# Down projection of a decoder block as seven-product visits, with the residual summed in HBM

## The chip, the cores and the metric

One core of a Trainium2 chip runs the whole kernel. The metric is device time in microseconds (us); lower is better. All arithmetic is float32 in the reference; on TensorE the kernel works with pairs of rounded float32 ("fp32r") values, hi and lo, whose sum is the number.

## What is computed

A decoder block on 512 tokens of 2048 channels: attention and a convolution branch, then a feed-forward part and a gated input. The change lies in the feed-forward's second product and reaches into the gate that follows it:

```python
h = _rmsnorm(x, g_ffn[l])
u = _causal_dwconv(h @ w_up[l], ffn_conv_w[l], ffn_conv_b[l])
ug, uv = jnp.split(u, 2, axis=-1)
x = x + (jax.nn.silu(ug) * uv) @ w_down[l]          # 512 x 5632 by 5632 x 2048
h = _rmsnorm(x, g_ple[l])
x = x + jax.nn.sigmoid(h @ w_ple_gate[l]) * (p[l].astype(x.dtype) @ w_ple_proj[l])
return _rmsnorm(x, g_final)
```

## The kernel before

Channels lie on the 128 partitions and tokens along the free axis, so a tile `a` is 128 channels x 512 tokens. The hidden layer has 44 such tiles (`hid`, kept in HBM), the residual 16 (`x1d` in HBM, `self.x1` in SBUF). `Kernel.run` takes a list of groups and issues their weight chunks one after the other. For each chunk it loads the raw weights on the SP queue into a pool of 7 buffers (`wraw`), up to 16 us of work ahead (`loads`), and cuts them one or two chunks ahead (`prep`): `cut` makes hi on ScalarE (line 268) and lo, the rest, on VectorE (line 269). `pump` gives the side work (evictions, statistics, hidden tiles) a turn after each chunk. A scheduler then sets the order of each engine's instructions; loads that go through `load` keep the program's order on SP.

An ordinary chunk (`Group`) is 256 rows by 512 columns of the weights: for 2 row blocks and 4 output tiles three matmuls of 512 tokens each, hi by hi, hi by lo and lo by hi (`products`, line 403), 24 in all.

The up projection runs as 44 `Pair`s. A pair is a 2 x 2 block product in seven products instead of eight (the Strassen-Winograd form): halves of the depth by two output tiles by halves of the tokens. `operands` makes the seven right-hand sides from two tiles. Each of them holds hi of 256 tokens in its left half and lo in its right, so a step takes one matmul of 512 columns (line 379) and one of 256 (line 380) per row block, eight row blocks per product. The seven weight operands come from `wraw`, from sums that were made in HBM beforehand (`s`), and from adding a further block by an accumulating transfer of GpSimd's queue (line 306).

The down projection (lines 948 to 951) is plain: four parts of 12, 12, 12 and 8 hidden tiles (`PARTS`), in each of which all 16 output tiles are made in four groups `mg`. `fetch` loads a part's hidden tiles and splits them into hi and lo, the first part beside the last pair, the next parts beside groups of the part before. `ready` loads the residual tiles `self.x1` in the first part; `ev_down` (line 945) adds each part's PSUM to them in SBUF on VectorE. The gate's first group then begins with `split_x1`, which makes hi and lo of every residual tile and the sum of squares, and ends in `stats`, whose result `rb3` the first eviction of the gate needs (line 1003). The last gate group is done in two halves of the tokens, so its matmuls have 256 columns.

Of the kernel before, what the change touches and what calls it, by code (L numbers as in the profile page):

```python
# [1 line left out]

# [15 lines left out]
P = 128  # L18
S = 512
# [40 lines left out]
class Group:  # L60


    def __init__(self, w, rhs, evict, tok=False, before=None, ns=ALL, keep=None):
        self.ns = ns
        self.w, self.rhs, self.evict, self.tok, self.before = w, rhs, evict, tok, before
        self.n = w.shape[0]
        self.nm = w.shape[3] // P
        self.keep = keep


class Pair:
# [9 lines left out]
    def __init__(self, src, rhs, evict, before=None, beside=()):  # L81
        self.src, self.rhs, self.evict, self.before, self.beside = src, rhs, evict, before, iter(beside)
        self.kh = src[1].shape[1]
        self.raw, self.cut, self.ps, self.c = {}, {}, {}, {}


class Kernel:
# [164 lines left out]
    def run(self, groups):  # L252
        nc = self.nc
        chunks = []
        for n, g in enumerate(groups):
            if not isinstance(g, Pair):
                chunks += [(g, c) for c in range(g.n)]
                continue
            if not isinstance(groups[n - 1], Pair):
                chunks.append((g, 5))  # L260
            after = groups[n + 1] if isinstance(groups[n + 1], Pair) else None
            chunks += [(after if p == 5 else g, p) for p in ORDER if p != 5 or after]
# [31 lines left out]
        def prep(i, kks=(slice(0, 2),)):  # L294
# [3 lines left out]
            if isinstance(g, Pair):  # L298
                hi = self.whi.tile([P, g.kh, P], F32R, tag="w", name="whi")
                lo = self.wlo.tile([P, g.kh, P], F32R, tag="w", name="wlo")  # L300
                raw = g.raw[{6: 5, 3: 5}.get(c, c)]
# [20 lines left out]

        loadx = self.start(dma, prep)
        begun.update(range(3))
        cuts = 1
        for i, (g, c) in enumerate(chunks):
# [8 lines left out]
            if g.before and c == (5 if isinstance(g, Pair) else 0):  # L335
                g.before()
            if isinstance(g, Pair):
                self.pair_step(g, c)
                for _ in range(2):
                    next(g.beside, None)  # L340
                self.pump()
                continue
# [10 lines left out]
            if c == g.n - 1:  # L353
                g.evict(g.ps)
            self.pump()
# [12 lines left out]
    def pair_step(self, g, c):  # L368
# [21 lines left out]
        if p == 4:  # L390
            g.evict(g.c[1], g.c[6], g.c[4], g.c[5])

# [237 lines left out]
    def build(self):  # L630
# [223 lines left out]
        def fold(c, eng):  # L854
            eng.tensor_tensor(c[:, LEFT], c[:, LEFT], c[:, RIGHT], op=ALU.add)

# [33 lines left out]
        F0 = [sum(PARTS[:i]) for i in range(len(PARTS))]  # L890
        hs = {}

        def fetch(pi):
            raw = {}
            for f in range(F0[pi], F0[pi] + PARTS[pi] + 2):
                if f < F0[pi] + PARTS[pi]:
                    raw[f] = self.A()
                    self.load(out=raw[f], in_=hid[f])
                if f - 2 >= F0[pi]:
                    hs[f - 2] = self.split(raw.pop(f - 2))  # L900
                yield


# [5 lines left out]

        def sums():  # L910
# [10 lines left out]
        builders = {0: fetch(0)}  # L921
        for j in range(KF):
            groups.append(Pair(srcs[j], lambda p, k: T2[p][k], ev_up(j), before=first_up if j == 0 else None,
                               beside=builders[0] if j == KF - 1 else ()))

        def ready(pi, mg):
            def f():
                if mg == 0:
                    if pi == 0:
                        self.finish_chains()  # L930
                    for _ in builders[pi]:
                        pass
                if pi == 0:
                    for m in range(4 * mg, 4 * mg + 4):
                        self.x1[m] = self.A()
                        self.load(out=self.x1[m], in_=x1d[m])
                if mg == 1 and pi + 1 < len(PARTS):
                    builders[pi + 1] = self.add_bg(fetch(pi + 1))
            return f

        def ev_down(mg):
            def f(ps):
                for m in range(4):
                    z = self.x1[4 * mg + m]
                    nc.vector.tensor_tensor(z, ps[m], z, op=ALU.add)
            return f

        for pi, n in enumerate(PARTS):
            for mg in range(4):
                groups.append(Group(t["w_down"][mg][F0[pi] // 2:(F0[pi] + n) // 2], lambda k, pi=pi: hs[F0[pi] + k],  # L950
                                    ev_down(mg), before=ready(pi, mg)))


        h2, pj = {}, {}

        def split_x1():
            for k in range(KD):
                h2[k] = self.split(self.x1[k], self.col(C_GPLE + k))
                self.nacc = self.square_add(self.x1[k], self.nacc)
                if k % 2:  # L960
                    yield
            yield from stats("rb3")()

        def begin_gate():
            self.g_split = self.add_bg(split_x1())
            next(self.g_split)
            next(self.g_split)

        def load_pj(mg):
            def f():  # L970
                if mg == 0:
                    begin_gate()
# [51 lines left out]
        for mg in range(4):  # L1024
            groups.append(Group(t["w_gate"][mg], lambda k: h2[k], ev_gate2(4 * mg, TOK_A if mg == 3 else ALL),
                                ns=TOK_A if mg == 3 else ALL, keep=kept if mg == 3 else None, before=load_pj(mg)))
        self.again = Group(t["w_gate"][3], lambda k: h2[k], lambda m, ps: ev_gate2(12 + m, TOK_B)([ps]), ns=TOK_B, keep=kept)
# [70 lines left out]
```

## Time and profile before

| | us |
|---|---|
| median of three runs | 2794.7 (2792.41 to 2795.51) |
| the profiled run, its own time | 2794.55 |
| span of that run, in which the engines work | 2792.8 |
| up projection, about | 1242 to 2108 in the span |
| down projection, about | 2108 to 2590 |
| gate, about | 2590 to 2779 |

TensorE (PE in the profile) is busy 99% of the span, VectorE (DVE) 62%, ScalarE (ACT) 41% and GpSimd (POOL) 6%. PEld is the loading of weights into TensorE, which runs beside its matmuls. Busy shares are means over unlike stages, so the stretches have to be read apart. The mean duration of one matmul is not what it costs, since each starts before the one ahead has ended; the price is the time of a long unbroken piece divided by its count. "Granted clock" is the part of TensorE's full speed that it had.

### The profile page before, as it was taken

To read this page: it belongs to the slowest core of one execution; us is meant where nothing else is said; L and a number is where in the kernel's file an instruction comes from. 1 tells how busy PE (TensorE), PEld (TensorE's weight loads), DVE (VectorE), ACT (ScalarE), POOL (GpSimd) and SP (SyncE) were. 2 spreads that over 40 slices of the span, in tenths; PEclk is the share of its full clock that TensorE was granted. 3 is DMA by queue.
4 is the path that set the end of the run, shared out by engine and by line. 5 is a ranking of instruction groups with operands and counts; after the bars stand their busy time and mean duration, and the time that the engine had idled before them with its cause. 6 is when DMAs were issued, how large, how long until landed. Compare 5 with 4: busy or idle time off the path is not lost.

```text
span 2792.8 us, 34852 instructions
## 1 busy us (share of the span) xinstructions
PE 2758.9 (99%) x13528; PEld 2323.2 (83%) x13528; DVE 1732.3 (62%) x2554; ACT 1138.2 (41%) x1647; POOL 166.2 (6%) x200
## 2 busy tenths in 40 slices
PE   9999999999999999999999999999999999999997
PEld 7888888888888888878888888888887888888787
DVE  5464588658646354478788887878876333335436
ACT  5354452222124233355555555555554221213323
POOL 0010110000000000000000000000000000000000
PEclk9999999999999999999999999999999999999998
DMA  8575756676666754366767676767666343323322
GB/s 275 162 226 141 225 149 195 195 197 183 195 195 190 197 156 162 147 203 183 212 190 209 193 206 192 208 198 198 206 198 249 121 143 102 124 94 110 98 95 95
DMA packets 152982, 489.84 MB, mean 175 GB/s; under 512 B 17136, under 2 KB 21232, under 8 KB 152816
## 3 DMA queue, kind: packets, MB, share of 16 engines
q1 hardware_dynamic: 127328, 395.32, 39.9%
q0 software_dynamic: 25344, 92.29, 18.8%
q8 instruction: 106, 1.74, 0.2%
q14 instruction: 60, 0.49, 0.1%
q10 hardware_dynamic: 144, 0.01, 0.0%
HBM read 457.14 MB, written 116.39 MB: 205 GB/s over the span
## 4 chain that ended last, share of the span: by engine, by line
PE 95%; DMA 2%; DVE 1%; ACT 1%; issue 0%; SPq 0%; POOL 0%; POOLq 0%; DVEq 0%; ACTq 0%
PE m L403 63%; PE m L379 20%; PE m L380 10%; DMA wraw<-w_up 1%; PE x L539 1%; PE x L512 0%; DMA wraw<-w_down 0%; PE x L513 0%; DVE wlo L269 0%; PE x L530 0%; ACT whi L268 0%; DMA wraw<-w_in 0%; SPq L116 0%; DVE o L1018 0%; DMA wraw<-w_proj 0%
## 5 line engine op out<-in xcount | busy, mean ns | idle before, releaser
L403 PE MATMUL m<-a,whi 128*128 128x512 f32 (+1 forms) x5056 | 1547.7, 388 | 11.0 <-ACT whi L268 5.0
L268 ACT ACTIVATE whi<-wraw 128x1024 fp32r<-128x1024 f32 (+1 forms) x637 | 667.8, 1057 | 1437.4 <-PE m L403 912.2
L269 DVE TENSOR_TENSOR wlo<-wraw,whi 128x1024 fp32r<-128x1024 f32 (+1 forms) x637 | 773.7, 1221 | 755.3 <-ACT whi L268 720.9
L403 PEld LDWEIGHTS m<-a,whi 128*128 128x128 f32 x5056 | 945.8, 188 | 203.1 <-ACT whi L268 5.4
L403 PE MATMUL m<-a,wlo 128*128 128x512 f32 (+1 forms) x2528 | 978.7, 388 | 0.0
L379 PE MATMUL m<-a,whi 128*128 128x512 f32 x2464 | 873.9, 400 | 3.5 <-ACT a L383 2.3
L380 PE MATMUL m<-a,wlo 128*128 128x256 f32 x2464 | 693.3, 281 | 0.8 <-DVE wlo L269 0.8
L379 PEld LDWEIGHTS m<-a,whi 128*128 128x128 f32 x2464 | 464.6, 189 | 120.4 <-ACT a L383 3.1
L403 PEld LDWEIGHTS m<-a,wlo 128*128 128x128 f32 x2528 | 475.8, 188 | 97.4 <-DVE wlo L269 1.1
L380 PEld LDWEIGHTS m<-a,wlo 128*128 128x128 f32 x2464 | 467.2, 190 | 1.3 <-DVE wlo L269 1.1
L596 DVE SCALAR_TENSOR_TENSOR a<-a,par 128x485 f32<-128x485 f32 (+19 forms) x240 | 172.4, 734 | 6.1 <-ACT a L593 1.6
L875 DVE SCALAR_TENSOR_TENSOR a<-a,par 128x511 f32<-128x511 f32 (+1 forms) x176 | 131.4, 747 | 1.7
L306 POOL DMA_DIRECT2D wraw<-w_up x88 | 76.3, 868 | 920.9 <-DVE a L868 712.9
L918 POOL DMA_DIRECT2D s<-w_up x88 | 72.7, 826 | 888.2 <-DMA s<-w_up 888.2
L383 ACT ACTIVATE a<-m 128x512 f32<-128x512 f32 x176 | 101.6, 578 | 0.4 <-PE m L380 0.4
L389 DVE TENSOR_TENSOR a<-m,a 128x512 f32<-128x512 f32 x44 | 30.4, 692 | 88.3 <-PE m L380 88.3
L403 PE MATMUL m<-whi,a 128*128 128x512 f32 x256 | 81.3, 392 | 0.0
L873 ACT ACTIVATE a<-a,par 128x512 f32<-128x512 f32 x88 | 71.0, 806 | 8.8 <-DVE a L870 8.0
L146 ACT ACTIVATE a<-a 128x512 fp32r<-128x512 f32 x88 | 53.8, 623 | 41.6 <-DVE a L224 21.6
L147 DVE TENSOR_TENSOR a<-a 128x512 fp32r<-128x512 f32 x88 | 59.3, 686 | 9.2 <-ACT a L146 9.0
L213 POOL TENSOR_TENSOR sm<-sm,mhalf 128x4 f32<-128x4 f32 (+1 forms) x14 | 15.4, 1102 | 804.5 <-DVE sm L212 797.1
L870 DVE TENSOR_TENSOR a<-a 128x512 f32<-128x512 f32 x88 | 60.2, 684 | 0.1
(132 smaller groups left out, 1274.9 us busy)
## 6 DMA issues: line engine op xcount, KB each, us to landing
wraw<-w_in SPq DMA_DIRECT2D x143, 512.0 KB, 4.5
wraw<-w_up SPq DMA_DIRECT2D x132, 512.0 KB, 6.6
s<-w_up SPq DMA_DIRECT2D x88, 512.0 KB, 5.7
s<-w_up POOLq DMA_DIRECT2D x88, 512.0 KB, 7.4
wraw<-s SPq DMA_DIRECT2D x88, 512.0 KB, 5.4
wraw<-w_up POOLq DMA_DIRECT2D x88, 512.0 KB, 6.1
wraw<-w_down SPq DMA_DIRECT2D x88, 512.0 KB, 3.5
wraw<-w_o SPq DMA_DIRECT2D x32, 512.0 KB, 6.9
```

The source lines that it names most:

```text
L268: nc.scalar.activation(hi, w, AF.Copy)
L269: nc.vector.tensor_tensor(lo, w, hi.bitcast(F32), op=ALU.subtract)
L306: nc.gpsimd.dma_start(out=raw, in_=g.src[{5: 1, 6: 2}[c]], accum_op=ALU.add)
L379: nc.tensor.matmul(ps, lhsT=hi[:, k], rhs=t, start=new and k == 0, stop=False, skip_group_check=True)
L380: nc.tensor.matmul(ps[:, LEFT], lhsT=lo[:, k], rhs=t[:, LEFT], start=False, stop=k == g.kh - 1, skip_group_check=True)
L383: nc.scalar.activation(x, ps, AF.Copy)
L403: nc.tensor.matmul(out, lhsT=l, rhs=r, start=first and n == 0, stop=last and n == 2)
L596: nc.vector.scalar_tensor_tensor(y[:, s:], u[:, :S - s], self.col(w + k), y[:, s:], op0=ALU.mult, op1=ALU.add)
L870: nc.vector.tensor_tensor(u, u, rb, op=ALU.mult)
L873: nc.scalar.activation(y, u, AF.Identity, scale=self.col(w + 2), bias=self.col(C_FB + ch))
L875: nc.vector.scalar_tensor_tensor(y[:, s:], u[:, :S - s], self.col(w + 2 - s), y[:, s:], op0=ALU.mult, op1=ALU.add)
L918: nc.gpsimd.dma_start(out=src[n], in_=w[h], accum_op=ALU.add)
```

## The change

The first six hidden tiles (`F0`) stay a plain product, in four groups of three chunks. The other 38 make 19 pairs of row blocks (`KP`), and for them the down projection is done in seven products. Eight pairs of output tiles (`o`) are visited in turn, and a visit takes its pair of outputs over a range of the 19 (`ENDS`, `VISITS`); the number of pairs in the range is called its depth below. There are 26 visits: a first round of depths 2, 3, 4, 5, 6, 7, 8, 8, the first three of them behind the second, third and fourth plain group, a second of depths 7 (seven times) and 8, a third of 8, 8, 8, 7, 6, 5, 4, 3, and at the end two of depth 2 and 1. The operands of a pair (`feed`, through the same `operands`) are made just before the first visit that needs them.

A visit's seven products (`NARROW`: 1, 5, 6, 2, 7, 3, 4) have outputs of 256 tokens, so `visit_step` issues three matmuls of 256 columns for each pair: hi by hi, hi by lo, lo by hi. The four weight blocks of the range are loaded, three sums are made by VectorE (lines 324, 326 and 328 of the changed kernel), and the last sum, for product 3, by an accumulating transfer on GpSimd's queue after product 6 has been cut (line 332). Products 1, 5, 6 and 4 are evicted by ScalarE and 2, 7 and 3 by VectorE.

The residual is no longer kept in SBUF. The plain groups (`ev_plain`, line 1024) and every visit but the last of each output pair (line 1055) add their result to `x1d` in HBM by accumulating transfers on GpSimd's queue, 16 and 36 of 256 KB. The last visit of a pair loads `x1d`, adds it (line 1044), splits the result for the gate and adds its squares (`chain`). The gate takes its rows in the order in which these visits end (`GATE_K`), and `stats` begins with the gate. The hooks of `fetch` and `feed` run with a delay of `LAG` steps.

```diff
-PARTS = [12, 12, 12, 8]
+F0 = 6
+KP = (KF - F0) // 2
+ENDS = [[2, 3, 4, 5, 6, 7, 8, 8], list(range(9, 17)), [min(n, KP) for n in range(17, 25)], [KP] * 2]
+VISITS = [(o, ENDS[r - 1][o] if r else 0, e) for r, es in enumerate(ENDS) for o, e in enumerate(es)]
+GATE_K = [m for o in (2, 3, 4, 5, 6, 7, 0, 1) for m in (2 * o, 2 * o + 1)]
+NARROW = [1, 5, 6, 2, 7, 3, 4]
...
+                if isinstance(g, Pair) and not g.wide:
+                    for h in {1: (0,), 5: (2, 3), 2: (1,)}.get(c, ()):
+                        g.raw[h] = self.wraw.tile([P, g.kh, P], F32, tag="w", name="wraw")
+                        self.load(out=g.raw[h], in_=g.src[h])
+                    return
...
+                if not g.wide:
+                    a = g.raw
+                    if c == 5:
+                        a["s"] = self.wraw.tile([P, g.kh, P], F32, tag="w", name="wraw")
+                        nc.vector.tensor_tensor(a["s"], a[2], a[3], op=ALU.add)
+                    elif c == 6:
+                        nc.vector.tensor_tensor(a["s"], a["s"], a[0], op=ALU.add)
+                    elif c == 7:
+                        nc.vector.tensor_tensor(a[2], a[2], a[0], op=ALU.add)
+                    cut(hi, lo, a[{1: 0, 2: 1, 7: 2, 4: 3}.get(c, "s")])
+                    g.cut[c] = hi, lo
+                    if c == 6:
+                        nc.gpsimd.dma_start(out=a["s"], in_=g.src[1], accum_op=ALU.add)
+                    return
...
+    def visit_step(self, g, c):
+        nc, p = self.nc, c
+        name = {1: "b", 6: "b", 7: "b", 4: "b", 2: "a", 5: "c", 3: "c"}[p]
+        new = name not in g.ps
+        if new:
+            g.ps[name] = self.mm.tile([P, S], F32, tag="m", name="m")
+        ps = g.ps[name][:, :H]
+        hi, lo = g.cut.pop(p)
+        for k in range(g.kh):
+            t = g.rhs(p, k)
+            for n, (w, x) in enumerate(((hi, LEFT), (hi, RIGHT), (lo, LEFT))):
+                nc.tensor.matmul(ps, lhsT=w[:, k], rhs=t[:, x], start=new and k == n == 0, stop=k == g.kh - 1 and n == 2,
+                                 skip_group_check=True)
+        if p in (1, 5):
+            g.c[p] = self.A()
+        if p in (1, 6, 5):
+            nc.scalar.activation(g.c[1 if p == 6 else p][:, LEFT if p == 1 else RIGHT], ps, AF.Copy)
+        elif p in (2, 3):
+            z = g.c[1][:, LEFT if p == 2 else RIGHT]
+            nc.vector.tensor_tensor(z, ps, z, op=ALU.add)
+        elif p == 7:
+            z = g.c[5][:, RIGHT]
+            nc.vector.scalar_tensor_tensor(z, ps, -1.0, z, op0=ALU.mult, op1=ALU.subtract)
+        else:
+            nc.scalar.activation(g.c[5][:, LEFT], ps, AF.Copy, scale=-1.0)
+            g.evict(g.c[1], g.c[5])
...
+        def ev_plain(mg):
+            def f(ps):
+                for m, x in enumerate(ps):
+                    z = self.A()
+                    nc.scalar.activation(z, x, AF.Copy)
+                    nc.gpsimd.dma_start(out=x1d[4 * mg + m], in_=z, accum_op=ALU.add)
+            return f
...
-                    z = self.x1[4 * mg + m]
-                    nc.vector.tensor_tensor(z, ps[m], z, op=ALU.add)
...
+            def before():
+                if end:
+                    for m in ms:
                         self.x1[m] = self.A()
                         self.load(out=self.x1[m], in_=x1d[m])
+            def chain(zs):
+                for m, z in zip(ms, zs):
+                    x = self.x1[m]
+                    nc.vector.tensor_tensor(x, z, x, op=ALU.add)
+                    h2[m] = self.split(x, self.col(C_GPLE + m))
                     yield
+                    self.nacc3 = self.square_add(x, self.nacc3)
+                    yield
+            def evict(*zs):
+                if end:
+                    self.chain(chain(zs))
+                else:
+                    for m, z in zip(ms, zs):
+                        nc.gpsimd.dma_start(out=x1d[m], in_=z, accum_op=ALU.add)
...
-                    begin_gate()
+                    self.finish_chains()
+                    self.nacc = self.nacc3
+                    self.g_split = self.add_bg(stats("rb3")())
```

The SP queue, where the last hidden tile is stored (`hid_17952` before, `hid_17916` after; `hid_11075` and so on are earlier hidden tiles, `x1d` residual tiles). Before:

```order
L116 DMA wraw<-w_down 128x1024
L116 DMA a<-hid_11819 128x512
L116 DMA a<-hid_12005 128x512
L116 DMA wraw<-w_down 128x1024
L116 DMA hid_17952<-a 128x512
L116 DMA a<-x1d_8346 128x512
L116 DMA a<-x1d_8353 128x512
L116 DMA a<-x1d_8688 128x512
L116 DMA a<-x1d_8695 128x512
L116 DMA wraw<-w_down 128x1024 x6
```

After:

```order
L126 DMA wraw<-w_down 128x1024 x3
L126 DMA hid_17916<-a 128x512
L126 DMA a<-hid_11075 128x512
L126 DMA a<-hid_11261 128x512
L126 DMA a<-hid_11447 128x512
L126 DMA a<-hid_11633 128x512
L126 DMA wraw<-w_down 128x1024 x2
```

The four residual loads behind the store are gone, hidden tiles for the new operands stand there instead, and three weight chunks now go out together ahead of it.

VectorE at the same place, from the last of the up projection's convolution on (the product that is stored is line 880 before and 944 after; 177 to 180 and 171, 174 are lines of `operands`). Before:

```order
L875 SCALAR_TENSOR_TENSOR a<-a,par 128x511
L875 SCALAR_TENSOR_TENSOR a<-a,par 128x510
L880 TENSOR_TENSOR a<-a 128x512
L269 TENSOR_TENSOR wlo<-wraw,whi 128x1024 x5
L945 TENSOR_TENSOR a<-m,a 128x512 x4
```

After:

```order
L944 TENSOR_TENSOR a<-a 128x512
L177 TENSOR_TENSOR a<-a 128x256
L178 TENSOR_TENSOR a<-a 128x256
L179 TENSOR_TENSOR a<-a 128x256
L180 TENSOR_TENSOR a<-a 128x256
L171 TENSOR_TENSOR a<-a 128x256 x3
L174 SCALAR_TENSOR_TENSOR a<-a 128x256
L171 TENSOR_TENSOR a<-a 128x256 x2
L177 TENSOR_TENSOR a<-a 128x256
L179 TENSOR_TENSOR a<-a 128x256
L171 TENSOR_TENSOR a<-a 128x256
L178 TENSOR_TENSOR a<-a 128x256
```

Behind the product stood the cuts of the next weight chunks; now 15 instructions on the operands stand there, of which these are the first 14, and the next cut (line 283) behind them.

GpSimd's queue where the up projection ends, before, and in the second round of visits, after (line 332 is the weight accumulate of a visit, 1055 the residual of the visit ahead of it). Before, these are the last rows of the queue:

```order
L213 TENSOR_TENSOR sm<-sm,mhalf 128x4
L306 DMA wraw<-w_up 128x1024 x85
L213 TENSOR_TENSOR sm<-sm,mhalf 128x4
L213 TENSOR_TENSOR sm<-sm,mhalf 128x2 x2
L1093 UNCONDITIONAL_BRANCH
L1093 ISA
```

After:

```order
L1055 DMA x1d_9377<-a 128x512
L1055 DMA x1d_8346<-a 128x512
L1055 DMA x1d_8353<-a 128x512
L332 DMA wraw<-w_down 128x896
L1055 DMA x1d_8688<-a 128x512
L1055 DMA x1d_8695<-a 128x512
```

Where GpSimd had no transfer left after the up projection, a weight accumulate now stands behind two residual accumulates in each visit.

VectorE at the end of the down projection (before: lines 150 and 248 split and square the residual in the gate's first chunks; after: the visit of depth 2, with 1044, 160 and 258 the residual of the visit before, 452 the eviction of that visit's product 3, 324 to 328 the sums). Before:

```order
L269 TENSOR_TENSOR wlo<-wraw,whi 128x1024 x2
L945 TENSOR_TENSOR a<-m,a 128x512 x3
L150 SCALAR_TENSOR_TENSOR a<-a,par 128x512
L945 TENSOR_TENSOR a<-m,a 128x512
L269 TENSOR_TENSOR wlo<-wraw,whi 128x1024
L248 TENSOR_TENSOR a<-a 128x512
L150 SCALAR_TENSOR_TENSOR a<-a,par 128x512
```

After:

```order
L452 TENSOR_TENSOR a<-m,a 128x256
L328 TENSOR_TENSOR wraw<-wraw 128x256
L283 TENSOR_TENSOR wlo<-wraw,whi 128x256
L1044 TENSOR_TENSOR a<-a 128x512
L326 TENSOR_TENSOR wraw<-wraw 128x256
L1044 TENSOR_TENSOR a<-a 128x512
L160 SCALAR_TENSOR_TENSOR a<-a,par 128x512
L283 TENSOR_TENSOR wlo<-wraw,whi 128x256
L258 TENSOR_TENSOR a<-a 128x512
L283 TENSOR_TENSOR wlo<-wraw,whi 128x256
L160 SCALAR_TENSOR_TENSOR a<-a,par 128x512
L283 TENSOR_TENSOR wlo<-wraw,whi 128x256
```

The residual's additions, splits and squares, which stood among cuts of 1024 elements, now stand among cuts and sums of 256 and 128.

## Rows read from the trace of the kernel before

**Rows 1.** The page: busy time of TensorE, and the chain by engine.

```profile
PE 2758.9 (99%) x13528; PEld 2323.2 (83%) x13528; DVE 1732.3 (62%) x2554; ACT 1138.2 (41%) x1647; POOL 166.2 (6%) x200
...
PE 95%; DMA 2%; DVE 1%; ACT 1%; issue 0%; SPq 0%; POOL 0%; POOLq 0%; DVEq 0%; ACTq 0%
```

**Rows 2.** Stretches of up and down projection (columns in the first line).

```profile
core 0: us, PE busy (x) PEld busy (x) DVE busy (x) ACT busy (x) POOL busy (x), PEclk, DMA share, GB/s
1640.00:1740.00 100.00, 100.00 (x568) 86.73 (x567) 80.36 (x106) 56.40 (x72) 8.65 (x10) 1.00 0.69 198
2140.00:2240.00 100.00, 100.00 (x442) 82.80 (x442) 38.71 (x43) 25.74 (x31) 0.00 (x0) 1.00 0.47 166
2440.00:2540.00 100.00, 100.00 (x443) 82.83 (x442) 35.40 (x38) 23.75 (x26) 0.00 (x0) 1.00 0.29 96
```

**Rows 3.** TensorE's waits, 1242 to 2098 us: releaser, total, times, longest.

```profile
PE m L379 <- ACT a L383: 2.3, 1, 2.3
PE m L379 <- ACT whi L268: 1.2, 1, 1.2
PE m L380 <- DVE wlo L269: 0.8, 1, 0.8
```

**Rows 4.** Chain (start, us, what, matmuls); then weight loads, ns least/median/most.

```profile
825.20 38.08 PE m L403 x168
...
2762.00 13.56 PE m L403 x113
...
L403 PEld LDWEIGHTS m<-a x192: 186/192/193, 2727.0 to 2772.3; 128*128 128x128 f32 x192
```

**Rows 5.** Timeline at the change from up to down, chain piece, then stretches.

```profile
2121.90 0.69 DVE L880 TENSOR_TENSOR a<-a 128x512 f32<-128x512 f32 x1
...
2122.62 0.32 SPq L116 DMA_DIRECT2D hid<-a  x1
2123.03 1.82 SPq L116 DMA_DIRECT2D a<-x1d  x4
2124.91 3.51 SPq L116 DMA_DIRECT2D wraw<-w_down  x6
...
2124.91 5.51 DMA wraw<-w_down
...
2131.62 1.22 PE L403 MATMUL m<-a,whi 128*128 128x512 f32 x2 [4.97 <-ACT whi L268]
...
2131.59 5.11 DVE L269 TENSOR_TENSOR wlo<-wraw,whi 128x1024 fp32r<-128x1024 f32 x4 [9.00 <-ACT whi L268]
...
2132.00:2136.00 4.00, 3.96 (x10) 2.62 (x10) 3.79 (x4) 2.98 (x3) 0.00 (x0) 0.52 1.02 407
2136.00:2140.00 4.00, 4.00 (x19) 3.34 (x18) 0.70 (x1) 0.66 (x1) 0.00 (x0) 1.00 1.05 392
```

**Rows 6.** TensorE at the end of the gate's first group, and that stretch.

```profile
2641.21 0.49 PE L181 MATMUL x<-a,onesr 128*128 128x512 f32 x1 [0.75 <-ACT a L146]
2641.94 0.49 PE L181 MATMUL x<-a,onesr 128*128 128x512 f32 x1 [0.23 <-DVE a L147]
2643.84 0.73 PE L403 MATMUL m<-a,whi 128*128 128x512 f32 x2 [1.41 <-DVE a L1003]
...
2644.00:2648.00 4.00, 4.00 (x11) 3.14 (x12) 4.00 (x8) 3.14 (x7) 0.00 (x0) 0.57 0.00 0
```

**Rows 7.** VectorE's timeline: like instructions in a row; one eviction of 256.

```profile
2096.83 2.36 DVE L269 TENSOR_TENSOR wlo<-wraw,whi 128x1024 fp32r<-128x1024 f32 x2
2099.10 0.75 DVE L875 SCALAR_TENSOR_TENSOR a<-a,par 128x511 f32<-128x511 f32 x1
2099.76 0.69 DVE L147 TENSOR_TENSOR a<-a 128x512 fp32r<-128x512 f32 x1
...
2109.53 2.49 DVE L147 TENSOR_TENSOR a<-a 128x512 fp32r<-128x512 f32 x4
...
2115.01 0.42 DVE L868 TENSOR_TENSOR a<-a 128x256 f32<-128x256 f32 x1
2115.35 0.42 DVE L869 TENSOR_TENSOR a<-a 128x256 f32<-128x256 f32 x1
...
2775.59 0.43 DVE a L1003
```

**Rows 8.** Transfers, us to landing: line 306 (512 KB), plain 128 KB, hidden tiles.

```profile
L306 POOL DMA_DIRECT2D wraw<-w_up x88: 862/862/933, 1214.8 to 2085.1; - x88
DMA to landing us min/median/max: 5.2/6.1/9.5
...
a<-a SPq DMA_DIRECT2D x48, 128.0 KB, 2.3
...
L116 SPq DMA_DIRECT2D a<-hid x44: 319/394/966, 2077.7 to 2408.8; - x44
DMA to landing us min/median/max: 2.0/3.3/8.2
```

More of the change, by code (lines that the diff above doesn't have):

```diff
@@ L258, in run @@
                 continue
-            if not isinstance(groups[n - 1], Pair):
+            if not g.wide:
+                chunks += [(g, p) for p in NARROW]
+                continue
+            near = [isinstance(x, Pair) and x.wide for x in (groups[n - 1], groups[n + 1])]
+            if not near[0]:
                 chunks.append((g, 5))
-            after = groups[n + 1] if isinstance(groups[n + 1], Pair) else None
+            after = groups[n + 1] if near[1] else None
             chunks += [(after if p == 5 else g, p) for p in ORDER if p != 5 or after]
@@ L334, in run @@
             tiles.pop(i, None)
-            if g.before and c == (5 if isinstance(g, Pair) else 0):
+            if g.before and c == ((5 if g.wide else 1) if isinstance(g, Pair) else 0):
                 g.before()
             if isinstance(g, Pair):
-                self.pair_step(g, c)
-                for _ in range(2):
-                    next(g.beside, None)
+                (self.pair_step if g.wide else self.visit_step)(g, c)
+                hooks.append(g)
+                while len(hooks) > (LAG if g.rate == 1 else 0):
+                    h = hooks.pop(0)
+                    for _ in range(h.rate):
+                        next(h.beside, None)
                 self.pump()
@@ L354, in run @@
                 g.evict(g.ps)
+            for _ in range(g.rate):
+                next(g.beside, None)
             self.pump()
@@ L887, in ev_up @@
             return f
[L890 to L901, printed above, removed]
         srcs = []
@@ L919, in sums, with feed, get @@
                     yield
-        builders = {0: fetch(0)}
+        def feed():
+            raw = {}
+            def get(i):
+                raw[i] = [self.A() for _ in range(2)]
+                for n, a in enumerate(raw[i]):
+                    self.load(out=a, in_=hid[F0 + 2 * i + n])
+            get(0)
+            for i in range(KP):
+                ops = self.operands(T3, i, *raw.pop(i))
+                for n in range(7):
+                    next(ops)
+                    if n == 0 and i + 1 < KP:
+                        get(i + 1)
+                    yield
@@ L922, in build, with fetch @@
+        hs = {}
+        def fetch():
+            raw = {}
+            for f in range(F0 + 2):
+                if f < F0:
+                    raw[f] = self.A()
+                    self.load(out=raw[f], in_=hid[f])
+                if f >= 2:
+                    hs[f - 2] = self.split(raw.pop(f - 2))
+                yield
+        fetcher, feeder = fetch(), feed()
         for j in range(KF):
+            last = j == KF - 1
             groups.append(Pair(srcs[j], lambda p, k: T2[p][k], ev_up(j), before=first_up if j == 0 else None,
-                               beside=builders[0] if j == KF - 1 else ()))
@@ L954, in build @@
[L954 to L960, printed above, removed]
-                    yield
[L962 to L967, printed above, removed]
+            def chain(zs):
[3 more added lines that the diff above has]
+                    h2[m] = self.split(x, self.col(C_GPLE + m))
+                    yield
+                    self.nacc3 = self.square_add(x, self.nacc3)
+                    yield
@@ new lines, in evict @@
+            def evict(*zs):
[4 more added lines that the diff above has]
+                        nc.gpsimd.dma_start(out=x1d[m], in_=z, accum_op=ALU.add)
+            more = max(0, 7 * VISITS[n + 1][2] - made[0]) if n + 1 < len(VISITS) else 0
+            made[0] += more
+            return Pair({h: t["w_down"][o, h][:, i:e] for h in range(4)}, lambda p, k: T3[p][i + k], evict, before,
+                        islice(feeder, more), wide=False)
@@ L969, in load_pj @@
+        made = [0]
+        n = 0
+        for mg in range(4):
+            groups.append(Group(t["w_down0"][mg], lambda k: hs[k], ev_plain(mg), before=ready(mg), beside=islice(feeder, 9), rate=3))
+            made[0] += 9
+            if mg:
+                groups.append(visit(n))
+                n += 1
+        groups += [visit(k) for k in range(n, len(VISITS))]
         def load_pj(mg):
```

53 lines of the change are left out of this document (27 added, 26 removed).

## The prediction

> **What bounds the kernel now.** I read the page's busy table and chain first: TensorE is busy 99% of the span and makes 95% of the chain [rows 1]. Next the stretches: in the up projection and in the down projection TensorE is busy in every microsecond at full clock, VectorE 80% in the first and 35 to 39% in the second [rows 2]. So a microsecond of matmul saved in the down projection is a microsecond of the run, if VectorE can take what the saving costs. The up projection is already made of seven-product steps, and TensorE's waits from 1242 to 2098 us sum to 4.3 us [rows 3]: 80% of VectorE, with two accumulating transfers for each pair, holds nobody up.
>
> The price of a matmul comes from unbroken pieces of the chain [rows 4]. 168 of 512 columns in 38.08 us are 226.7 ns each; 113 of 256 columns, each with a weight load of its own (the last group, half of the tokens), in 13.56 us are 120.0 ns each.
>
> **Part 1, TensorE's work.** Removed: 22 chunks x 4 groups x 24 = 2112 matmuls of 512 columns, 2112 x 0.2267 = 478.8 us. In their place stand 3 x 4 x 24 = 288 plain ones, 65.3 us, and 19 pairs of rows x 8 output pairs x 7 products x 3 = 3192 of 256 columns, 3192 x 0.1200 = 383.0 us. That is 448.3 us: **-30.5 us**. Seven products for eight would give 1/8 of the 38/44 that are changed; a third of a step more in matmul starts (three of 256 for one of 512 and one of 256) takes part of it back.
>
> The Trainium skill (TensorE: Matmul & The Clock Gate, Part 3, on what overlaps) lets a weight load overlap a running matmul only if it goes to another row group, which speaks against 256 columns with a full load each. By its 128 columns at 1.2 GHz a load would add some 107 ns to each matmul here, an estimate from that page. The trace doesn't agree: [rows 4] have loads of 192 ns beside matmuls that start every 120 ns.
>
> **Part 2, the change from up to down.** Before, TensorE waits 4.97 us at 2126 to 2131 for the fifth plain chunk and then runs at half clock to 2136: 0.52 granted in the four microseconds from 2132, 1.00 after [rows 5]. The reason is the SP queue: the store of the last hidden tile waits for VectorE (2121.90), four loads of the residual stand next, and the weight load goes out at 2124.91 and lands 5.51 later. After, six of the twelve hidden tiles are no longer split there (6 x 0.62 = 3.7 us of VectorE ahead of that product), so the store goes at some 2118.5. Four hidden loads stand behind it (4 x 0.46), and the weights leave at 2120.6 and land near 2126. But their cut on VectorE now stands behind 15 instructions of the new operands, which wait for hidden tiles loaded behind the same store: store 2118.5 + 0.4 + 3.3 for a 256 KB load [rows 8] = 2122.3, 15 x 0.34 = 5.1, cut 1.14: 2128.6 for 2132.8 before. **-4 us**. Bounds: -7 (no wait, no half clock) to +3 (a hidden load takes 8.2, its longest, and cancels the rest).
>
> **Part 3, the gate's first group.** Before, the residual's square sums begin with the gate, and the scale comes late: TensorE waits 0.75 + 0.23 + 1.41 = 2.4 us, then runs at 0.57 clock for four microseconds, 1.7 lost [rows 6]. After, the sums are made during the last visits, and the statistics begin 5 chunks of 5.44 us earlier. **-4 us**, bounds -4 to 0.
>
> **Part 4, VectorE in the middle visits.** Starts of like instructions in a row [rows 7] give 0.34 us for 256 elements, 0.60 to 0.62 for 512, 1.14 for 1024: about 0.07 + 0.00105 per element, so 0.20 for 128 and 1.00 for 896. 512 with a scale take 0.67. A visit of depth 7 needs seven cuts and three sums of 896 (10.0), three evictions of 256 (1.1) and 11 operand instructions (3.7): 14.8 us against 7 x 7 x 0.360 = 17.6 on TensorE, 84%; depth 8: 16.2 of 20.2, 80%. That is the level of the up projection, where nothing waited. ScalarE has fewer of these pieces than VectorE. On SP a visit puts four weight loads and two hidden loads, 6 x 0.46 = 2.8 us of 17.6; the residual that the last visits load was accumulated eight visits, some 140 us, before. Both I cost at nothing; if that cover went, it would show as rival 2 does. What is new is GpSimd's queue: the weight accumulate of a visit now stands behind two 256 KB accumulates into HBM, the second of which waits for the last eviction of the visit before. Counted from the end of that visit's product 3, depth 7: product 4 2.5, eviction with its place in the queue 0.8, two issues of 0.86: the weight accumulate leaves at 5.0. Its cut must be done when product 3 is due, at 2.5 + 5 x 2.52 = 15.1. With 1.95 for the two halves of the cut there are 8.2 us for a landing that took 5.2 to 9.5, median 6.1 [rows 8]. Some visits will wait a little; the same at depth 5, and TensorE's waits at the short first visits. I take **+4 us** for these 22 visits; 0 where all landings are like the median, +18 where each is a microsecond too late.
>
> **Part 5, the short visits at the end.** Depths 4, 3, 2 and 1 give TensorE 10.1, 7.6, 5.0 and 2.5 us each. VectorE must, in each, do ten pieces of the depth, three evictions, and the end of the residual of the visit before (2 x (0.60 + 0.67 + 0.60) = 3.74): 10.8, 9.5, 8.2 and 6.8 us. For depths 4 and 3 that is the bound, counted from product 3 to product 3 (TensorE 10.4 and 7.9): +0.9 with gaps, and +1.6. For depths 2 and 1 it is a chain: eviction of product 3, VectorE's rows up to the cut of product 6 (0.36 + 0.34 + 0.34 + 0.60 + 0.34 + 0.60 + 0.67 + 0.34 = 3.6; 3.0 for depth 1), accumulate, cut on both engines (0.8; 0.5), product 3 (0.7; 0.4). For the accumulate of 64 and 128 KB no row stands. Below it are plain loads of 128 KB with 2.3, above it 6.1 for 512 KB [rows 8]; I take 3.7, nearer to the small one, with the 0.86 of the issue and half a microsecond of adding. Then 3.6 + 3.7 + 0.8 + 0.7 + gaps 0.6 = 9.4 against 5.4 of TensorE, +4.0; and 7.7 against 2.9, +4.8. The gate's first cut stands behind the last eviction and two residual sums (0.2 + 0.5 + 0.36 + 1.2 + 1.14 = 3.4, less 0.7 + 0.2 of TensorE): +2.5. Together 13.8. Waits of 4 to 5 us cost half clock afterwards in [rows 5], so +3 for that: **+17 us**. Lower end: accumulates cost nothing beyond VectorE's own rows (2.8 + 4.0 + 1.6 + 0.4 + 1.5) and the clock holds: +10. Upper end: accumulates land in 9.5, 5.8 later in each of the last two visits and 4 in all in the two before, +16: +33.
>
> The Trainium skill (DMA: Bandwidth & Descriptors, anatomy of an SWDGE transfer) has 2.0 us plus bytes at 436 GB/s. That is an estimate of 2.2 us for 64 KB, and the tail would be some 3 us shorter; for 512 KB it says 3.2 where the trace has 5.2 at least.
>
> **Sum**, on the profiled run of 2794.55 (span 2792.8 and 1.75 around it; the runs' median is 2794.7): -30.5 - 4 - 4 + 4 + 17 = -17.5, **2777 us**.
>
> **Rivals.**
> 1. *The tail takes all that its upper end allows*, +33 for +17: 2793, no change that shows. For it: ScalarE and VectorE run in order, so a late accumulate stops the next visit's cuts as well. Against it: no weight traffic but 64 to 256 KB is left there.
> 2. *The weight accumulates land late in every visit*: slower. Place: GpSimd's queue behind the two residual accumulates. The point is 8.2 us for a landing; beyond it each microsecond costs 19 visits of depth 5 and more about 18 us. At 9.7 us the sum is 2777 - 4 + 1.5 x 18 = 2800, and at 10.5 it is 2814. For it: the residual's accumulates share the queue, and 9.5 is on record in the up projection. Against it: the DMA queues move no more bytes a microsecond than there (some 3.5 MB in a visit of 17.6 us, 200 GB/s, against 198).
> 3. *The short visits overlap*: landings near 2.3, half clock nowhere, the middle without waits: 2777 - 7 - 4 - 3 = 2763.
> 4. *Weight loads pace the short matmuls*: at the 192 ns of the load rows, 3192 x 0.072 = +230 us, 3007. [Rows 4] show the same pattern without it. (It is what the rule of the Trainium skill, TensorE: Matmul & The Clock Gate, Part 3, would bring.)
>
> **How the numbers follow.** My sum 0.60 (2766 to 2787), rival 1 0.14, rival 2 0.13, rival 3 0.12, rival 4 0.01. A measurement of this kernel can tell about 0.2% from no change: faster is below 2789, slower above 2800. Faster: 0.60 + 0.12 + 0.02 of rival 1 = 0.74. Same: the rest of rival 1 and a hundredth of rival 2, 0.13. Slower 0.13. The range keeps the sum, most of rival 1 and half of rival 3: 2763 to 2795.
>
> **What would show it.** Right: matmuls of 256 columns 120 ns apart in the visits; full busy and clock 1.00 in the middle; the wait near 2126 halved and the one near 2641 gone; and in the last 25 us before the gate TensorE idle a third to a half of the time, released by the cuts of products 3. VectorE near 84% from 2200 to 2500. Wrong: waits on the cut of product 3 in every middle visit (rival 2), a step of 8 x 3 matmuls that takes more than 2.9 us (rival 4), or a tail whose waits come from another step.

## The result and the profile after

The changed kernel takes 2852.9 us (median of four runs, 2850.5 to 2855.1) for 2793.6 before: a ratio of 1.0214, 95% interval 1.0201 to 1.0226. It is slower, by 59 us; the forecast was 2777, faster. The profiled execution took 2850.68 us, with a span of 2848.9.

The page of after, busy time of the engines, which answers to [rows 1]:

```profile
PE 2758.2 (97%) x14896; PEld 2388.3 (84%) x14896; DVE 1912.8 (67%) x2939; ACT 1257.9 (44%) x1968; POOL 234.6 (8%) x278
```

TensorE is busy as long as before (2758.9), although its work was cut, and now idles 2848.9 - 2758.2 = 90.7 us, for 33.9 before. So the question has two halves: what TensorE waits for, and why the shorter work takes as long. The sum of TensorE's waits in the whole span (releaser, total, times, longest) answers the first; its four longest groups:

```profile
PE m L444 <- ACT a L449: 51.7, 19, 5.5
PE m L444 <- ACT whi L282: 7.2, 5, 2.9
PE m L470 <- ACT a L905: 3.8, 1, 3.8
PE m L418 <- ACT a L422: 3.6, 2, 2.8
```

Line 444 are the visits' matmuls, line 449 ScalarE's evictions of products 1, 5 and 6, line 282 ScalarE's half of the cut. The stretches of the middle visits, to be held against [rows 2], answer the second:

```profile
core 0: us, PE busy (x) PEld busy (x) DVE busy (x) ACT busy (x) POOL busy (x), PEclk, DMA share, GB/s
2200.00:2300.00 100.00, 87.81 (x679) 87.00 (x679) 66.57 (x96) 41.53 (x73) 10.69 (x13) 0.93 0.63 158
2300.00:2400.00 100.00, 86.51 (x661) 85.49 (x661) 64.86 (x102) 42.35 (x78) 13.20 (x15) 0.91 0.59 149
2400.00:2500.00 100.00, 85.25 (x647) 84.43 (x647) 62.81 (x96) 39.86 (x72) 10.46 (x12) 0.91 0.60 153
```

TensorE idles 12 to 15% of the time and the granted clock is 0.91 to 0.93, where it was 1.00; VectorE is at 63 to 67%, far from full. Two visits of depth 7 show how a wait comes about. First ScalarE's queue, then GpSimd's, then TensorE (in brackets, idle time before the row and what ended it; TensorE's row at 2360.65 belongs to the visit between the two):

```profile
2326.55 0.38 ACT L449 ACTIVATE a<-m 128x256 f32<-128x256 f32 x1
2326.83 0.41 ACT L170 ACTIVATE a<-a 128x256 fp32r<-128x256 f32 x1
2335.20 0.95 ACT L282 ACTIVATE whi<-wraw 128x896 fp32r<-128x896 f32 x1 [7.96 <-DMA wraw<-w_down]
2336.06 0.70 ACT L170 ACTIVATE a<-a 128x256 fp32r<-128x256 f32 x2
2336.67 0.36 ACT L449 ACTIVATE a<-m 128x256 f32<-128x256 f32 x1
...
2382.20 0.95 ACT L282 ACTIVATE whi<-wraw 128x896 fp32r<-128x896 f32 x1 [5.44 <-DMA wraw<-w_down]
2383.05 0.71 ACT L170 ACTIVATE a<-a 128x256 fp32r<-128x256 f32 x2
2383.66 0.36 ACT L449 ACTIVATE a<-m 128x256 f32<-128x256 f32 x1
```

```profile
2322.33 0.86 POOL L1055 DMA_DIRECT2D x1d<-a  x1 [17.71 <-DVE a L452]
2324.54 0.88 POOL L1055 DMA_DIRECT2D x1d<-a  x1 [1.34 <-ACT a L457]
2325.39 0.94 POOL L332 DMA_DIRECT2D wraw<-w_down  x1
...
2373.26 1.06 POOL L332 DMA_DIRECT2D wraw<-w_down  x1
```

```profile
2331.27 0.28 PE L444 MATMUL m<-a,wlo 128*128 128x256 f32 x1
2337.08 0.80 PE L444 MATMUL m<-a,whi 128*128 128x256 f32 x2 [5.53 <-ACT a L449]
...
2360.65 0.80 PE L444 MATMUL m<-a,whi 128*128 128x256 f32 x2 [3.28 <-ACT a L449]
...
2380.79 0.28 PE L444 MATMUL m<-a,wlo 128*128 128x256 f32 x1
2384.08 0.80 PE L444 MATMUL m<-a,whi 128*128 128x256 f32 x2 [3.01 <-ACT a L449]
```

A visit runs its products in the order 1, 5, 6, 2, 7, 3, 4. Product 7 is added onto product 6 in the same PSUM tile (`b` in `visit_step`), so it starts when product 6 has been evicted. On ScalarE that eviction (2336.67) stands behind the cut of product 3 (2335.20), which stands there idle for 7.96 us until the accumulating weight transfer has landed. The engine takes its instructions in order: product 6 was done some 2.5 us before TensorE stopped at 2331.55, and its eviction ran 5.1 us after that stop. So the transfer isn't due when product 3 is, but one product earlier, when product 7 is.

The Trainium skill (PSUM — Partial Sum Buffer, Engine vs sequencer instructions) says that the queue of ScalarE is strictly first in, first out. These rows agree: a ready eviction of 0.36 us waits behind a cut that isn't ready.

How late the transfer is can be read off. In the first visit it leaves at 2325.39, and the cut starts 9.8 us later; from the cut's start to the eviction's end are 1.8 us, and product 7 was due 6.2 after the issue, so there were 4.3 us for it, and it was 5.5 late: TensorE waited 5.53. In the other visit there were 7.8 - 1.8 = 6.0 us, it took 8.9, and TensorE waited 3.01. The visit between them had 5.9, took 9.1, and waited 3.28. Landings of line 332 from 2280 to 2510 us (least, median, most):

```profile
DMA to landing us min/median/max: 6.2/8.7/10.0
```

For [rows 8] the same kind of transfer had a median of 6.1. With 8.7 for some 5.4 allowed (the mean of the three visits), a visit is 3.3 us late. Fifteen such waits outside the last short visits sum to 47.8 us in the trace (51.7 less the 3.9 of four waits from 2608 on), 3.2 each.

Each wait has a second price. Four stretches of 4 us around the middle one of the three visits:

```profile
2356.00:2360.00 4.00, 1.37 (x12) 1.17 (x10) 1.06 (x2) 2.04 (x4) 0.00 (x0) 0.95 0.17 49
2360.00:2364.00 4.00, 3.35 (x15) 3.35 (x16) 3.97 (x11) 3.08 (x8) 0.00 (x0) 0.50 0.44 123
2364.00:2368.00 4.00, 4.00 (x27) 4.00 (x26) 3.90 (x7) 0.95 (x1) 0.00 (x0) 0.69 0.33 107
2368.00:2372.00 4.00, 4.00 (x35) 4.00 (x35) 2.90 (x5) 1.18 (x3) 0.86 (x1) 1.00 0.17 12
```

After a wait of 3.28 us the granted clock is 0.50 (1.2 GHz), then 0.69, then 1.00 (2.4 GHz). That is where the saved TensorE work went: from 2125 to 2600 us TensorE is busy 426.0 us at a granted clock of 0.94, so the clock lacks some 26 us there.

### The profile page after: what moved, and what is told of

The parts are those of the page before. It is cut to its first block, busy times and chain, and to the rows that moved or that the text cites. A ratio compares the mean times of both kernels' runs of the same rounds, so it can differ in the third digit from the quotient of the medians.

```text
span 2848.9 us, 38714 instructions
## 1 busy us (share of the span) xinstructions
PE 2758.2 (97%) x14896; PEld 2388.3 (84%) x14896; DVE 1912.8 (67%) x2939; ACT 1257.9 (44%) x1968; POOL 234.6 (8%) x278
## 5 line engine op out<-in xcount | busy, mean ns | idle before, releaser
L282 ACT ACTIVATE whi<-wraw 128x1024 fp32r<-128x1024 f32 (+7 forms) x743 | 735.2, 999 | 1355.9 <-PE m L470 591.1
L283 DVE TENSOR_TENSOR wlo<-wraw,whi 128x1024 fp32r<-128x1024 f32 (+7 forms) x743 | 849.1, 1150 | 631.2 <-ACT whi L282 604.7
L470 PE MATMUL m<-a,whi 128*128 128x512 f32 (+1 forms) x3840 | 1171.8, 387 | 6.2 <-ACT a L905 3.8
L470 PEld LDWEIGHTS m<-a,whi 128*128 128x128 f32 x3840 | 716.5, 188 | 151.1 <-ACT a L905 4.2
L470 PE MATMUL m<-a,wlo 128*128 128x512 f32 (+1 forms) x1920 | 740.1, 386 | 0.0
L419 PE MATMUL m<-a,wlo 128*128 128x256 f32 x2464 | 692.4, 281 | 0.5 <-DVE wlo L283 0.5
L418 PEld LDWEIGHTS m<-a,whi 128*128 128x128 f32 x2464 | 464.7, 189 | 123.5 <-ACT a L422 6.7
L444 PE MATMUL m<-a,whi 128*128 128x256 f32 x2128 | 410.9, 296 | 59.6 <-ACT a L449 51.7
L419 PEld LDWEIGHTS m<-a,wlo 128*128 128x128 f32 x2464 | 467.4, 190 | 1.3 <-DVE wlo L283 1.0
L470 PEld LDWEIGHTS m<-a,wlo 128*128 128x128 f32 x1920 | 361.2, 188 | 72.5 <-DVE wlo L283 0.2
L444 PEld LDWEIGHTS m<-a,whi 128*128 128x128 f32 x2128 | 352.0, 203 | 65.9 <-ACT a L449 56.1
L444 PE MATMUL m<-a,wlo 128*128 128x256 f32 x1064 | 311.7, 294 | 0.0
L444 PEld LDWEIGHTS m<-a,wlo 128*128 128x128 f32 x1064 | 215.6, 203 | 0.3 <-DVE wlo L283 0.3
```

The source lines that it names most:

```text
L282: nc.scalar.activation(hi, w, AF.Copy)
L283: nc.vector.tensor_tensor(lo, w, hi.bitcast(F32), op=ALU.subtract)
L418: nc.tensor.matmul(ps, lhsT=hi[:, k], rhs=t, start=new and k == 0, stop=False, skip_group_check=True)
L419: nc.tensor.matmul(ps[:, LEFT], lhsT=lo[:, k], rhs=t[:, LEFT], start=False, stop=k == g.kh - 1, skip_group_check=True)
L444: nc.tensor.matmul(ps, lhsT=w[:, k], rhs=t[:, x], start=new and k == n == 0, stop=k == g.kh - 1 and n == 2, skip_group_check=True)
L470: nc.tensor.matmul(out, lhsT=l, rhs=r, start=first and n == 0, stop=last and n == 2)
```

## The experiments

Three theories went into the first four runs. **A**: TensorE waits at product 7, because the eviction of product 6 stands behind the cut of product 3, and that cut waits for a transfer which the two residual accumulates ahead of it hold up. **B**: the accumulating transfer of the weights is that slow by itself. **C**: VectorE has too much to do in a visit. In the table, idle is the span less TensorE's busy time, both from the pages. Each ratio is to runs of the kernel before made beside that run: their median is 2793.6 us for the kernel after, 2791.6 for the first four experiments and 2793.1 for the last two.

| kernel | median us | ratio to before (95%) | TensorE busy | TensorE idle |
|---|---|---|---|---|
| before | 2793.6 | | 2758.9 | 33.9 |
| after | 2852.9 | 1.0214 (1.0201 to 1.0226) | 2758.2 | 90.7 |
| e1_order | 2800.7 | 1.0033 (1.0021 to 1.0045) | 2738.9 | 59.8 |
| e2_weights_first | 2817.3 | 1.0097 (1.0080 to 1.0113) | 2741.9 | 70.2 |
| e3_no_residual | 2819.1 | 1.0089 (1.0061 to 1.0116) | 2744.3 | 71.5 |
| e4_vector_sum | 2762.9 | 0.9897 (0.9882 to 0.9912) | 2726.9 | 32.4 |
| e5_order_first | 2780.2 | 0.9951 (0.9935 to 0.9968) | 2736.4 | 43.8 |
| e6_vec_order | 2762.7 | 0.9886 (0.9868 to 0.9905) | 2726.0 | 34.7 |

Against e4_vector_sum, which has the same 14896 matmuls, after idles 58.3 us more and is busy 31.3 us more: the waits and what the clock takes behind them.

**The place of the cut.** The preparation of product 3 begins one step later, and its cut is issued behind the eviction of product 6. No transfer and no other eviction is touched.

```diff
-                    cut(hi, lo, a[{1: 0, 2: 1, 7: 2, 4: 3}.get(c, "s")])
+                    if c == 3:
+                        with self.tc.issue_after(g.ev6.ins):
+                            cut(hi, lo, a["s"])
+                    else:
+                        cut(hi, lo, a[{1: 0, 2: 1, 7: 2, 4: 3}.get(c, "s")])
...
-            while cuts < min(i + (3 if isinstance(g, Pair) else 2), len(chunks) - 1):
+            while cuts < min(i + (3 - (not g.wide and c == 6) if isinstance(g, Pair) else 2), len(chunks) - 1):
...
-            nc.scalar.activation(g.c[1 if p == 6 else p][:, LEFT if p == 1 else RIGHT], ps, AF.Copy)
+            e = nc.scalar.activation(g.c[1 if p == 6 else p][:, LEFT if p == 1 else RIGHT], ps, AF.Copy)
+            if p == 6:
+                g.ev6 = e
```

> Only ScalarE's order in the visits is changed: the cut of product 3, which waits for the weight accumulate, is put behind the eviction of product 6 instead of ahead of it (and is prepared one step later). Theory A (TensorE waits at product 7 for that eviction, because the cut ahead of it waits for a transfer that is delayed by two residual accumulates): the 51.7 us of waits on ScalarE's evictions fall below 15 us, what is left waits on the cut of product 3 itself, since the transfer is as late as before (8.9 us in the middle); time about 2810 (2790 to 2830). Theory C (VectorE has too much to do in the visits): no change, 2850.

It took 2800.7 us: 52 of the 59 lost us are back with no transfer changed (50 by the two ratios to before). TensorE's waits in the visits (from 2125 us on):

```profile
PE m L448 <- ACT whi L282: 16.4, 14, 3.4
PE m L448 <- DVE wlo L283: 6.2, 11, 0.8
PE m L448 <- DVE a L461: 4.3, 9, 0.6
PE m L448 <- ACT a L453: 1.5, 4, 0.5
```

The waits for ScalarE's evictions fell from 51.7 to 1.5. From 2125 to 2540 us, ahead of the short visits, what is left is 7.3 us for ScalarE's half of the cut (the other 9.1 of the 16.4 lie in the short visits), 6.2 for VectorE's half, and 4.3 for VectorE's eviction of product 7 (line 461), which product 4 needs. That eviction stands behind the late cut on VectorE, as product 6's did on ScalarE: at 2323.02 us in one visit, behind cuts that began at 2319.34 after 3.89 us of waiting. The transfer lands no sooner, 9.1 in the median from 2280 to 2510 us, which is past the 8.2 us that the prediction allowed for this place. The ordering half of theory A holds.

**The queue ahead of the transfer.** Each weight accumulate is issued ahead of the two residual accumulates of the visit before, which are held back until then.

```diff
-                        nc.gpsimd.dma_start(out=a["s"], in_=g.src[1], accum_op=ALU.add)
+                        w = nc.gpsimd.dma_start(out=a["s"], in_=g.src[1], accum_op=ALU.add)
+                        with self.tc.issue_after(w.ins):
+                            for m, z in self.held:
+                                nc.gpsimd.dma_start(out=self.x1d[m], in_=z, accum_op=ALU.add)
+                        self.held = []
...
-                    for m, z in zip(ms, zs):
-                        nc.gpsimd.dma_start(out=x1d[m], in_=z, accum_op=ALU.add)
+                    self.held = list(zip(ms, zs))
```

> Only GpSimd's queue is changed: each visit's weight accumulate now stands ahead of the two residual accumulates of the visit before, same transfers, same sizes. Theory A (the weight accumulate is late because of the two ahead of it): its landing in the middle falls from 8.9 to 5 to 6.5 us and it leaves some 1.7 us sooner; waits on ScalarE's evictions below 15 us; time about 2790 (2775 to 2805). Theory B (an accumulate of 450 KB into SBUF is that slow beside the weight loads, whatever stands ahead): landing stays at 8 to 9, time above 2830. Theory C (VectorE): 2850.

And the residual accumulates of the visits left out altogether, so that the residual lacks what these visits add:

```diff
-                    for m, z in zip(ms, zs):
-                        nc.gpsimd.dma_start(out=x1d[m], in_=z, accum_op=ALU.add)
+                    pass
```

> The 36 accumulates of the visits' results into the residual in HBM are left out (the residual misses these parts), all else stands. Theory A: the weight accumulate lands in 5 to 6.5 us in the middle, waits on the evictions below 12 us, time 2775 to 2795, like the run with the weights first or a little less. Theory B: landing stays at 8 to 9 us, time above 2830.

The two agree with each other, at 2817.3 and 2819.1 us. The landings of the weight accumulate from 2280 to 2510 us, first with it ahead, then with no residual accumulates:

```profile
DMA to landing us min/median/max: 4.9/6.5/9.9
```

```profile
DMA to landing us min/median/max: 5.2/6.8/9.1
```

So the company of the residual costs the transfer 2 us, no more. With no accumulate ahead of it, it takes 6.5 to 6.8, little more than in the up projection. The waits for evictions shrink and don't go, first with it ahead, then with no residual accumulates:

```profile
PE m L448 <- ACT a L453: 30.0, 16, 4.5
```

```profile
PE m L444 <- ACT a L449: 31.8, 18, 3.4
```

Both times miss what was expected: theory A named 2805 at most for the first and 2795 for the second, theory B more than 2830. Theory A also had the transfer leave some 1.7 us sooner. Against its deadline it doesn't: the transfer overwrites what the cut of product 6 reads, so its issue now waits for VectorE's half of that cut (e2_weights_first, at 2310.23, 2331.22 and 2352.68 us), and product 7 leaves it 5.1, 5.0 and 4.3 us in these three visits, where the cut of product 3 began 7.4, 6.2 and 7.8 us after the issue. Neither A nor B is the whole cause: taking the queue away takes 20 to 22 of the 51.7 us of these waits, the smaller part; e1_order, with the queue as it was, takes away all but 1.5.

**No transfer.** The last weight sum is made by VectorE; the 26 accumulates of line 332 are gone.

```diff
+                    elif c == 3:
+                        nc.vector.tensor_tensor(a["s"], a["s"], a[1], op=ALU.add)
...
-                    if c == 6:
-                        nc.gpsimd.dma_start(out=a["s"], in_=g.src[1], accum_op=ALU.add)
```

> The last weight sum (for product 3) is made by VectorE from the block that is loaded anyway, the 26 weight accumulates go; VectorE gets about 26 additions more (1.0 us each at depth 7, 84% to 90% busy in the middle). Theories A and B (the accumulate is what TensorE waits for, by way of ScalarE's order): the waits on the evictions go, time 2770 to 2795. Theory C (VectorE has too much to do): slower than the changed kernel, above 2855.

2762.9 us, 90 less than after, and 1.0% faster than before. It lies 7 us below the 2770 to 2795 that theories A and B named; the short visits lose their accumulates too, and their cost falls from 17.3 to 6.3 us (Part 5 below). Its middle visits (columns as in the first stretches above):

```profile
2200.00:2300.00 100.00, 100.00 (x836) 100.00 (x835) 86.07 (x124) 51.74 (x89) 10.38 (x12) 1.00 0.60 161
2300.00:2400.00 100.00, 100.00 (x836) 100.00 (x835) 92.38 (x145) 55.30 (x102) 9.54 (x11) 1.00 0.60 169
2400.00:2500.00 100.00, 100.00 (x835) 100.00 (x834) 86.66 (x117) 53.36 (x87) 6.08 (x8) 1.00 0.52 145
```

In these stretches TensorE is never idle and keeps its full clock, with VectorE at 86 to 92%, more than after asks of it. Theory C falls. From 2125 to 2540 us TensorE waits 0.4 us in all.

**Both remedies together, and a check on the place.** The edits of e1_order and e2_weights_first in one kernel; and those of e4_vector_sum and e1_order in one. Their diffs are the ones above.

> The two edits of e1_order and e2_weights_first together: the cut of product 3 stands behind the eviction of product 6 on ScalarE, and each weight accumulate stands ahead of the two residual accumulates on GpSimd. Theory A (the loss is a deadline, product 7's instead of product 3's, met by a transfer that two residual accumulates hold up): the landing stays at the 6.5 us median of e2_weights_first while the deadline is back at product 3 with its 8.2 us, so TensorE's waits on the cuts of the middle visits fall under 10 us in all and the time to 2770 to 2785. Theory B (the accumulating transfer of 450 KB is itself too slow for either place): waits of 20 us or more stay and the time is 2798 or more, no better than e1_order alone.

> The sum for product 3 by VectorE, as in e4_vector_sum, and the cut of product 3 behind the eviction of product 6 on ScalarE, as in e1_order. Theory A: with no transfer to wait for, the place of the cut no longer matters, so the time is that of e4_vector_sum, 2763 within 3 us. Rival (the eviction behind the cut costs something whatever the cut waits for): under 2758. Theory C in a weaker form (VectorE, 92% busy there, has no room for a cut that starts later): TensorE waits on VectorE's half of the cut of product 3 and the time is over 2768.

The first took 2780.2 us. The landing is 6.5 again (4.9 to 9.2), the deadline is back at product 3, and the waits for ScalarE's half of the cut fall from 16.4 to 8.3; ahead of the short visits (2125 to 2540 us) they fall from 7.3 to 0.3:

```profile
PE m L452 <- ACT whi L282: 8.3, 7, 3.0
PE m L452 <- DVE a L465: 3.6, 8, 0.6
PE m L452 <- DVE wlo L283: 1.7, 3, 0.6
PE m L452 <- ACT a L457: 1.6, 4, 0.5
```

Neither edit alone beats the kernel before; the two together do, by 0.5%, with the accumulating transfer kept. TensorE is busy 97.2, 97.9 and 99.0% in the three stretches from 2200 to 2500, at clock 1.00. That settles theory A as a matter of a deadline: in the middle visits a landing of 6.5 us is late for product 7 and in time for product 3, nearly always. The 8.0 us that are left lie in the short visits.

The second took 2762.7 us, the time of e4_vector_sum. Where nothing late stands in the cut, its place on ScalarE is free. So it was neither the order alone nor the transfer alone, but a late operand in front of a ready eviction.

The best version is e4_vector_sum, with e6_vec_order its equal: one more sum of 896 elements on VectorE per visit for the transfer. By trace, e5_order_first lies behind it in two stretches. From 2500 to 2600 us it is busy 89.6 at clock 0.93, for 95.3 at 0.98, and in the middle visits it is idle 5.8 us. Together that is some 16 us (95.3 x 0.98 less 89.6 x 0.93 is 10.1, and 5.8) of the 17 between the medians.

## Why the prediction was wrong, part by part

**Part 1, TensorE's work: right.** The visits' matmuls start every 120 ns: 836 in 100 us in the rows above. TensorE's busy time fell by 32.0 us from before to e4_vector_sum, for 30.5 worked out. The rival on weight loads is out, and with it what the rule of the Trainium skill (TensorE: Matmul & The Clock Gate, Part 3) would have brought: the loads of 192 ns lie beside the matmuls here too.

**Part 2, the change from up to down: right in kind, better in size.** The wait of 4.97 us in [rows 5] for a weight chunk is gone; what stands there now is 0.7 us for the eviction of a plain group (first fence, TensorE's waits), and no half clock follows (second, the stretch around it):

```profile
PE m L470 <- ACT a L1023: 0.7, 1, 0.7
```

```profile
2120.00:2140.00 20.00, 19.28 (x88) 15.75 (x87) 13.97 (x36) 12.12 (x29) 6.00 (x8) 1.00 1.04 314
```

That is -4.3, and -1.9 for the four microseconds at 0.52: -6 for the forecast -4, within its bounds.

**Part 3, the gate's first group: right.** The waits of [rows 6] are gone; the gate begins at some 2650, and the 100 us from 2660 show no idle time:

```profile
2660.00:2760.00 100.00, 100.00 (x443) 82.83 (x442) 46.47 (x67) 37.37 (x49) 1.03 (x1) 1.00 0.37 120
```

**Part 4, the middle visits: the step that failed.** It said +4; after shows some +80. By difference: 2850.7 less (2794.6 - 30.5 - 6 - 4 + 17 = 2771). Three things went wrong in it, in this order of weight.

The deadline was put at the wrong product. The step counted from the end of one product 3 to the next and gave the transfer 8.2 us. It took for granted that a late cut holds up only its own product. It dismissed ScalarE because it "has fewer of these pieces than VectorE", which is its load and not its order, and didn't ask what is queued behind the cut there, though the tail's rival names just that ("a late accumulate stops the next visit's cuts as well"). The order of ScalarE's instructions, which can be read before any run, has the eviction of product 6 there. The allowance was 4.3 to 6.0 us. e1_order, which moves only this, took back 52 us.

The landing was taken from the up projection, a median of 6.1. In the visits it was 8.7, and 6.5 with nothing ahead of it. By rival 2's own price, 8.7 for 8.2 would have been 9 us.

The half clock was left out of the step. Part 5 counted it for waits of 4 to 5 us, Part 4 and rival 2 for none. Over e4_vector_sum, after pays 31.3 us of busy time for 58.3 of idle, about half a microsecond for each.

VectorE's share was right: e5_order_first, with the same work and few waits, has 79 to 81% in the middle for 80 to 84 worked out.

**Part 5, the short visits: right in the sum, +17, partly by luck.** From 2610 to 2650 after is idle 12.2 us, and the clock is 0.91 and 0.82 there and 0.92 up to 2670; the busy time of each stretch times what the clock lacks gives 5.1. That is +17.3:

```profile
2610.00:2630.00 20.00, 16.96 (x127) 16.55 (x126) 16.28 (x33) 10.08 (x23) 0.86 (x1) 0.91 0.44 116
2630.00:2650.00 20.00, 10.84 (x64) 8.91 (x63) 15.01 (x37) 11.90 (x31) 1.72 (x2) 0.82 0.74 237
2650.00:2670.00 20.00, 20.00 (x82) 16.39 (x83) 11.62 (x17) 8.74 (x11) 0.00 (x0) 0.92 0.77 254
```

The sum holds two misses that cancel: idle time 12.2 for 13.8, and the clock 5.1 for 3. At depths 4 and 3 the waits of 1.3 and 1.8 us, for 0.9 and 1.6, aren't VectorE's work: they are for the eviction of product 6 behind the late cut, as in the middle. The chain forecast for depths 2 and 1 is there, with waits on the cuts of products 6 and 3: depth 2 waits 2.7 us for 4.0, depth 1 5.1 for 4.8, the gate 1.4 for 2.5. (The 7.7 in the term of depth 1 lacks the gaps of 0.6 that the 9.4 of depth 2 has; with them it is 8.2.)

The accumulates of 256, 192, 128 and 64 KB landed in 4.0, 3.8, 3.5 and 4.6 us, for 3.7 taken between two bounds. The Trainium skill (DMA: Bandwidth & Descriptors, anatomy of an SWDGE transfer) has a fit by which 2.2 us for 64 KB is an estimate; the 4.6 measured decides against that here. In e4_vector_sum, without the accumulates, the same end costs 4.7 us of idle time and 1.6 of clock, 6.3 (its stretches from 2530 to 2570). The lower bound of +10, which was called VectorE's own rows, was too high, for VectorE even makes one more sum in each of these visits.

**The rivals.** Rival 2 was the right mechanism at the wrong point: the weight accumulates are late in nearly every visit, from about 5.4 us on and not from 8.2. Rival 3 named 2763 for a run whose middle has no waits and whose short visits overlap. e4_vector_sum, without the accumulates, has such a middle and took 2762.9; but it is another kernel, its short visits still cost 6.3 us, and so close an agreement is luck.

## What to carry to other kernels

When a step waits for a transfer, its deadline isn't set by the work that uses the result alone: an instruction that stands behind the waiting one on the same engine, and that somebody else needs sooner, sets an earlier one (here product 7's, 2.5 us before product 3's). So print the queue of the engine that waits, and look there for evictions. A share of 44% busy on ScalarE says nothing against that. And a wait of 3 us that returns in every round is to be priced with the half clock that followed it here; the waits of up to 0.6 us in the middle of e5_order_first left the clock at 1.00.

## What the runs showed of the hardware

An accumulating transfer of 448 or 512 KB into SBUF took 6.5 to 6.8 us in the median with no accumulate ahead of it (e2_weights_first, e3_no_residual) and 8.7 behind two accumulates of 256 KB into HBM on the same queue (after). One each of 256, 192, 128 and 64 KB took 4.0, 3.8, 3.5 and 4.6, so in these four the time doesn't fall with the size. Waits of 3 us, repeated every 24 us, cost half as much again in granted clock (31.3 us of busy time on 58.3 of idle, after against e4_vector_sum): 0.50 in the four microseconds after one, 0.69 in the next four. 256 columns with a weight load each held 119.6 ns a matmul for 300 us on end, at full clock, with VectorE at 86 to 92% (e4_vector_sum).
